# The second feed-forward product by the seven-product scheme at two levels, computed transposed, with operand sums on GpSimd

## The chip, the cores and the metric

The kernel runs on one core of a Trainium2 chip. The metric is the device time of one execution in microseconds (us). The engines are TensorE (PE, with its weight loads PEld), VectorE (DVE), ScalarE (ACT), GpSimd (POOL) and SyncE (SP), whose queue issues nearly all DMAs.

## The reference

One layer of an encoder on x of 2048 tokens x 1024 channels, all float32:

```
h   = rmsnorm(x, g_mix);  p = h @ w_in
y_f = rmsnorm(re(fft2 of 8 groups of 64 channels of p), g_fourier)
y_h = rmsnorm(hyena_mix(the other channels of p), g_hyena)      # two gated long convolutions
x   = x + concat(y_f, y_h) @ w_out
hm  = rmsnorm(x, g_mlp)
a   = square(relu(hm @ w_fc1))        # 2048 x 4096
x   = x + a @ w_fc2                   # 4096 x 1024
out = rmsnorm(x, g_final)
```

The change concerns `x + a @ w_fc2` and the last norm.

## The kernel before

The stages follow one another: input projection, Fourier and long convolutions, output projection, first feed-forward product (`fc1`), second (`fc2`). A scheduler orders the instructions of each engine by data and by the order in which the code is written; each engine then runs its list in order and waits on semaphores. SP's list holds the loads in the order in which they are issued.

A float32 product is made of three matmuls (`mm3`): each operand is split into a high part of reduced precision and the rest, `hi = cast(x)` on ScalarE and `lo = x - hi` on VectorE (`split`), and hi*hi + lo*hi + hi*lo are summed in PSUM.

Both feed-forward products use the seven-product scheme of two-by-two blocks, which saves one product in eight for some sums of blocks. In `fc2` the tokens are taken in two blocks of 1024 (`blk`). In each, the blocks of the scheme are two halves of 512 tokens, two halves of the 4096 inner channels and two halves of 512 output columns. The products are called `m1` to `m7`. The sums of `a` are made by `fc1` and stored in DRAM (`ad[blk][n]`, a0m1 to a1m7 in the trace), those of `w_fc2` were made early in the kernel (`td`). `fc2` therefore only loads: `fetch` brings tiles `ra` (128 x 1024) and `rb` (128 x 1024), eight steps ahead; `prepare` splits each into qah, qal, qbh, qbl (L196, L197); `use` multiplies. The tokens are the stationary side (128 x 128) and 512 output columns the moving one. The result p2u, p2m or p2v is added to the residual `acc` (L1374), and `finish` applies the norm and stores. GpSimd works in this stage only at the very end (L1345), and `fc1` begins its first two products (`begun`) while it ends.

Of the kernel before, what the change touches and what calls it, by code (L numbers as in the profile page):

```python
# [10 lines left out]
F32 = mybir.dt.float32  # L11
FR = mybir.dt.float32r
BF16 = mybir.dt.bfloat16
# [3 lines left out]
EPS = 1e-5  # L17
# [117 lines left out]
def hybrid_block(ctx: ExitStack, tc: tile.TileContext, A, out):  # L135
# [5 lines left out]
    def scratch(name, shape):  # L141
        return dram.tile(shape, F32, tag=name, name=name)
# [12 lines left out]
    ad = [{n: scratch(f"a{i}{n}", [16, P, 512]) for n in ORDER} for i in range(2)]  # L155

    td = scratch("td", [P, 16, 4, 512])

    cpool = ctx.enter_context(tc.tile_pool(name="cpool", bufs=1))
    ps = ctx.enter_context(tc.tile_pool(name="ps", bufs=2, space=PSUM))  # L160
# [6 lines left out]
    def psum(name):  # L167

        banks["stack"].close()
        banks["other"] = banks["stack"].enter_context(tc.tile_pool(name=name, bufs=1, space=PSUM, reuse_waits="tile"))  # L170
        banks["two"] = name == "psd"

    def pa(nm):
        banks["n"] += 1
# [33 lines left out]
    def mm3(o, lh, ll, rh, rl, start, stop, more=False):  # L208

        a = nc.tensor.matmul(o, lhsT=lh, rhs=rh, start=start, stop=False, skip_group_check=more)  # L210
        nc.tensor.matmul(o, lhsT=lh, rhs=rl, start=False, stop=False, skip_group_check=more)  # L211
        return a, nc.tensor.matmul(o, lhsT=ll, rhs=rh, start=False, stop=stop, skip_group_check=more)  # L212
# [946 lines left out]
    def fc2_rows(blk, n, g):  # L1159

        f, f2 = slice(2 * g, 2 * g + 2), slice(2 * g + 16, 2 * g + 18)
        b = {
            "m1": w2v[:, f, left],
            "m2": w2v[:, f2, left],
            "m3": w2v[:, f2, right],
            "m4": td[:, f, 2],
            "m5": td[:, f, 0],
            "m6": td[:, f, 3],
            "m7": td[:, f, 1],
        }  # L1170
        return ad[blk][n][f].rearrange("f p t -> p f t"), b[n]

    def fc2_product(p, j, a, b, start):
        tk = slice(128 * j, 128 * j + 128)
        for g in range(2):
            mm3(p, a[0][:, g, tk], a[1][:, g, tk], b[0][:, g, :], b[1][:, g, :], start and g == 0, g == 1, not start)

    def fc1(mp, rp, zp, b, first, following, begun):

# [103 lines left out]
        fc2_begun = {}  # L1283
        for i, n in enumerate(("m1", "m2")):
            parts = []
            for j, v in enumerate(fc2_rows(0, n, 0)):
                t = rp[:, 2 * i + j, :].rearrange("p (f c) -> p f c", f=2)
                nc.sync.dma_start(t, v)
                parts.append((zf[:, 4 * i + 2 * j], zf[:, 4 * i + 2 * j + 1]))
                split(*parts[j], t)  # L1290
            fc2_begun[n] = [pa("p2" + "um"[i]) for _ in range(4)]
            for j, p in enumerate(fc2_begun[n]):
                fc2_product(p, j, *parts, True)
        return fc2_begun

    def fc2(mp, blk, gfin, begun):

        out_t = out.rearrange("(p t) d -> p t d", t=NT)

        todo = {  # L1300
            "m1": ("u", True, (0, 0)),
            "m2": ("m", True, (0, 0)),
            "m6": ("u", False, (0, 1)),
            "m5": ("v", True, (1, 1)),
            "m3": ("v", False, (0, 1)),
            "m7": ("u", False, (1, 1)),
            "m4": ("u", False, (1, 0)),
        }
        steps = [(g, n, e) for g in range(4) for n in todo for e in range(2)]
        if begun:  # L1310
            steps = [(0, n, e) for e in range(2) for n in ("m1", "m2")] + steps[4:]
        held, raws, parts, acc = {}, {}, {}, {}

        def fetch(k):
            if k < len(steps) and not (begun and k < 2):
                g, n, e = steps[k]
                raws[k] = [load(mp, tag, [P, 2, 512], v, bufs) for (tag, bufs), v in zip((("ra", 10), ("rb", 11)), fc2_rows(blk, n, 2 * g + e))]

        def prepare(k):
            if k in raws:  # L1320
                parts[k] = []
                for side, t in zip("ab", raws.pop(k)):
                    hl = [mp.tile([P, 2, 512], FR, tag="q", name=f"q{side}{h}{steps[k][1]}", bufs=16) for h in "hl"]
                    split(*hl, t)
                    parts[k].append(hl)

        def residual(t0):
            for t in range(t0, t0 + 4):
                acc[t] = load(mp, "acc", [P, 1024], x2d[:, 8 * blk + t, :], 12)

        junk = mp.tile([P, 1024], BF16, tag="mjunk", name="mjunk")

        def finish(i):
            t = acc[i]
            r = rms(t, 1024, junk, "o")
            nc.vector.scalar_tensor_tensor(out=t, in0=t, scalar=r, in1=gfin, op0=ALU.mult, op1=ALU.mult)
            nc.sync.dma_start(out_t[:, 8 * blk + i, :], t)

        ssq = {}

        def squares(i, c):

            s = small.tile([P, 1], F32, tag="ssq", name="ssq_l")
            nc.scalar.activation(junk[:, c], acc[i][:, c], AF.Square, accum_out=s)
            nc.gpsimd.tensor_mul(acc[i][:, c], acc[i][:, c], gfin[:, c])  # L1345
            return s

        def finish_last(i):
            s, v = squares(i, left), small.tile([P, 1], F32, tag="var", name="v_l")
            nc.vector.tensor_add(s, s, ssq[i])  # L1350
            nc.vector.tensor_scalar(out=v, in0=s, scalar1=1.0 / 1024, scalar2=EPS, op0=ALU.mult, op1=ALU.add)
            r = rsqrt(v, small, "s")
            for c, queue in ((right, nc.scalar), (left, nc.sync)):
                t = acc[i][:, c]
                if queue is nc.scalar:
                    nc.scalar.mul(t, t, r)
                else:
                    nc.vector.tensor_scalar(out=t, in0=t, scalar1=r, scalar2=None, op0=ALU.mult)
                queue.dma_start(out_t[:, 8 * blk + i, c], t)

        def use(k, j):
            g, n, e = steps[k]
            bank, start, (rows, cols) = todo[n]
            if k in parts:
                if start and e == 0:
                    held[bank, j] = pa(f"p2{bank}")
                fc2_product(held[bank, j], j, *parts[k], start and e == 0)
            else:
                held[bank, j] = begun[n][j]
            if e == 0:  # L1370
                return
            i = j + 4 * rows
            t = acc[i][:, 512 * cols : 512 * cols + 512]
            nc.vector.tensor_add(t, t, held[bank, j])  # L1374
            if g == 3 and blk == 1 and i in (6, 7):

                if n == "m7":
                    ssq[i] = squares(i, right)
                elif n == "m4":
                    finish_last(i)  # L1380
            elif g == 3 and n in ("m3", "m4"):
                finish(i)

        AHEAD = 8
        with tc.high_priority(offset=300):
            for k in range(5 if begun else 4):
                fetch(k)
            residual(0)
            for k in range(5 if begun else 4, AHEAD):
                fetch(k)  # L1390
            for k in range(4):
                prepare(k)
        tail = 4 if blk else 0
        for k in range(len(steps) - tail):
            fetch(k + AHEAD)
            prepare(k + 2)
            if k == 3:
                residual(4)
            for j in range(4):
                use(k, j)  # L1400
            yield

        for k in range(len(steps) - tail, len(steps)):
            prepare(k)
        for j in range(5 if tail else 0):
            for k, t in ((len(steps) - 4, j), (len(steps) - 3, j), (len(steps) - 2, j - 1), (len(steps) - 1, j - 1)):
                if 0 <= t < 4:
                    use(k, t)
        yield

    def run(*steps):
# [106 lines left out]
        zstack.close()  # L1518
    with pool("fc2") as mp:

        mp.tile([P, 2, 512], F32, tag="ra", name="ra", bufs=10)
        mp.tile([P, 2, 512], F32, tag="rb", name="rb", bufs=11)
        mp.tile([P, 2, 512], FR, tag="q", name="q", bufs=16)
        mp.tile([P, 1024], BF16, tag="mjunk", name="mjunk")
        mp.tile([P, 1024], F32, tag="gfin", name="gfin")
        mp.tile([P, 1024], F32, tag="acc", name="acc", bufs=12)
        gfin = load(mp, "gfin", [P, 1024], A["g_final"].broadcast_to([P, 1024]))
        for blk in range(2):
            run(fc2(mp, blk, gfin, {} if blk else begun))


# [42 lines left out]
```

## Time and profile before

| what | value |
|---|---|
| runs | 2251.12, 2251.25, 2245.84 us; median 2251.12 |
| the profiled execution | 2246.41 us, span 2244.6 us |
| busy in the span | PE 2193.4 us (98%), DVE 1472.5 (66%), ACT 1075.1 (48%), POOL 770.8 (34%) |
| the second product | from 1620.2 us to the end |

In a row of groups stand line, engine, operation, out<-in, shapes, count, then busy us, mean ns of one, and idle time ahead of them with what ended it. In a row of the timeline stand start (us), length (us), engine, line, operation. Lengths include time in which the instruction waits inside the engine. Matmuls overlap, so their distance, not their length, is their cost.

### The profile page before, as it was taken

How to read it: one execution, taken by the hardware profiler on the slowest of the kernel's cores; microseconds unless marked ns; L12 is line 12 of the kernel's file. 1: busy time of each engine (PE TensorE's matmuls, PEld its weight loads, DVE VectorE, ACT ScalarE, POOL GpSimd, SP SyncE). 2: the span in 40 equal slices, each digit the busy share in tenths (PEclk: the TensorE clock that was granted, in tenths of full speed). 3: DMA queues.
4: the chain of work that ended last, by engine and by line, in shares of the span. 5: the costliest groups of instructions: out<-in, count | busy, mean ns of one | idle time of the engine just before them, and what ended most of it. 6: DMA issues, size and time to landing. Idle time of an engine off the chain costs nothing.

```text
span 2244.6 us, 34527 instructions
## 1 busy us (share of the span) xinstructions
PE 2193.4 (98%) x12881; PEld 1794.5 (80%) x12881; DVE 1472.5 (66%) x2196; ACT 1075.1 (48%) x1788; POOL 770.8 (34%) x583
## 2 busy tenths in 40 slices
PE   8999899999999999999999999999999999999998
PEld 6888788676888778887888878888888888888886
DVE  7998767775788864566444474444477666866667
ACT  6555211354556645556555565555443333533333
POOL 3444332454366501337555556555200000000000
PEclk9999999999999999999999999999999999999999
DMA  7535897669898756586444475444498756866631
GB/s 268 178 132 171 313 320 254 208 227 336 304 306 257 237 154 180 175 270 192 153 154 155 155 248 162 150 153 155 160 369 298 248 190 190 308 196 188 200 110 75
DMA packets 289081, 477.00 MB, mean 213 GB/s; under 512 B 17605, under 2 KB 133519, under 8 KB 284177
## 3 DMA queue, kind: packets, MB, share of 16 engines
q1 hardware_dynamic: 282961, 459.34, 61.4%
q10 hardware_dynamic: 5952, 15.46, 2.1%
q8 instruction: 101, 1.65, 0.3%
q14 instruction: 67, 0.55, 0.1%
HBM read 313.56 MB, written 168.00 MB: 215 GB/s over the span
## 4 chain that ended last, share of the span: by engine, by line
PE 89%; ACT 3%; DVE 3%; POOL 2%; issue 2%; DMA 1%; SPq 0%; ACTq 0%; POOLq 0%; DVEq 0%
PE p2u L212 5%; PE p2u L211 5%; PE p2u L210 5%; PE pu L211 5%; PE pu L212 5%; PE pu L210 5%; PE p1u L210 5%; PE p1u L212 5%; PE p1u L211 5%; PE pk L667 3%; PE p2v L211 3%; PE p2v L212 3%; PE p2v L210 3%; PE pz L779 2%; PE p1v L210 2%; PE p1v L211 2%
## 5 line engine op out<-in xcount | busy, mean ns | idle before, releaser
L196 ACT CAST qahm<-ra 128x1024 fp32r<-128x1024 f32 x110 | 115.9, 1053 | 346.7 <-PE p2u L211 172.0
L197 DVE TENSOR_TENSOR qalm<-ra,qahm 128x1024 fp32r<-128x1024 f32 x110 | 134.6, 1224 | 154.7 <-ACT qahm L196 151.8
L1345 POOL TENSOR_TENSOR acc<-acc,gfin 128x512 f32<-128x512 f32 x4 | 5.1, 1277 | 631.6 <-DMA out<-acc 624.4
L211 PE MATMUL pu<-wl,xh 128*128 128x512 f32 x512 | 200.9, 392 | 6.9 <-DVE wl L197 6.5
L210 PE MATMUL pu<-wh,xh 128*128 128x512 f32 x512 | 203.7, 398 | 1.0 <-ACT wh L199 1.0
L212 PE MATMUL pu<-wh,xl 128*128 128x512 f32 x512 | 200.7, 392 | 0.0
L211 PE MATMUL p2u<-qblm,qahm 128*128 128x512 f32 x504 | 196.1, 389 | 0.0
L210 PE MATMUL p2u<-qbhm,qahm 128*128 128x512 f32 x504 | 195.9, 389 | 0.0
L212 PE MATMUL p2u<-qbhm,qalm 128*128 128x512 f32 x504 | 195.8, 389 | 0.0
L197 DVE TENSOR_TENSOR qblm<-rb,qbhm 128x1024 fp32r<-128x1024 f32 x110 | 134.0, 1218 | 0.8 <-ACT qbhm L196 0.7
L412 POOL TENSOR_TENSOR acc<-acc,cw 128x512 f32<-128x512 f32 x45 | 59.8, 1330 | 196.0 <-DVE acc L389 192.6
L196 ACT CAST ahm<-s 128x512 fp32r<-128x512 f32 x124 | 76.8, 621 | 100.2 <-PE p1v L211 54.8
L197 POOL TENSOR_TENSOR alm<-W,ahm 128x512 fp32r<-128x512 f32 x63 | 88.8, 1410 | 92.2 <-ACT ahm L196 92.2
L211 PEld LDWEIGHTS pu<-wl,xh 128*128 128x128 f32 x512 | 97.0, 189 | 28.3 <-DVE wl L197 6.9
L196 ACT CAST qbhm<-rb 128x1024 fp32r<-128x1024 f32 x110 | 115.4, 1049 | 3.1 <-DMA rb<-in_w_fc 1.9
L210 PEld LDWEIGHTS pu<-wh,xh 128*128 128x128 f32 x512 | 96.8, 189 | 22.1 <-ACT wh L199 1.8
L212 PEld LDWEIGHTS pu<-wh,xl 128*128 128x128 f32 x512 | 96.7, 189 | 20.6 <-DVE xl L197 0.6
L210 PEld LDWEIGHTS p2u<-qbhm,qahm 128*128 128x128 f32 x504 | 94.6, 188 | 20.1 <-issue 0.3
L211 PEld LDWEIGHTS p2u<-qblm,qahm 128*128 128x128 f32 x504 | 94.6, 188 | 19.6
L212 PEld LDWEIGHTS p2u<-qbhm,qalm 128*128 128x128 f32 x504 | 94.6, 188 | 19.4
L210 PE MATMUL p1u<-bm,ahm 128*128 128x512 f32 x252 | 99.0, 393 | 4.6 <-ACT ku L1207 4.6
L196 ACT CAST ahm<-W 128x512 fp32r<-128x512 f32 x94 | 58.1, 621 | 94.7 <-PE p1u L211 90.6
(376 smaller groups left out, 6141.6 us busy)
## 6 DMA issues: line engine op xcount, KB each, us to landing
W<-in_w_fc SPq DMA_DIRECT2D x66, 512.0 KB, 4.7
ks<-spec SPq DMA_DIRECT2D x64, 512.0 KB, 4.7
rb<-td SPq DMA_DIRECT2D x64, 512.0 KB, 10.9
ra<-a1m SPq DMA_DIRECT2D x56, 512.0 KB, 3.7
ra<-a0m SPq DMA_DIRECT2D x54, 512.0 KB, 3.8
rb<-in_w_fc SPq DMA_DIRECT2D x46, 512.0 KB, 5.2
f<-in_w_fc SPq DMA_DIRECT2D x16, 1024.0 KB, 8.5
td<-f SPq DMA_DIRECT2D x16, 1024.0 KB, 5.9
```

Of the source, the lines that this page charges most:

```text
L196: nc.scalar.copy(hi, src)
L197: (eng or nc.vector).tensor_sub(lo, src, hi)
L210: a = nc.tensor.matmul(o, lhsT=lh, rhs=rh, start=start, stop=False, skip_group_check=more)
L211: nc.tensor.matmul(o, lhsT=lh, rhs=rl, start=False, stop=False, skip_group_check=more)
L212: return a, nc.tensor.matmul(o, lhsT=ll, rhs=rh, start=False, stop=stop, skip_group_check=more)
L412: nc.gpsimd.tensor_add(m1, m1, cw[:, 3, :])
L667: ordered(nc.tensor.matmul(p[:, 128 * j : 128 * j + 128], lhsT=f2[:, 4 * q + j, :], rhs=self.G[:, :, 4 * q + j], start=True, stop=True))
L779: nc.tensor.matmul(p[:, 256 * sp : 256 * sp + 256], lhsT=e1[:, sp, :], rhs=zz[:, :, lo : lo + 16], start=True, stop=True)
L1345: nc.gpsimd.tensor_mul(acc[i][:, c], acc[i][:, c], gfin[:, c])
```

## The change

`fc2` applies the scheme twice. The seven products of before are now the inner ones, called `inner`: for each, the operands are no longer multiplied, but cut in two-by-two blocks again: tokens by `blk` (0 or 1, 512 each), inner channels into two halves of 1024, output columns into two halves of 256. Each inner product takes seven outer products (`outer`), 49 in all. The tiles of an inner product are h11, h21 (block 0, first and second half of its channels), h12, h22 (block 1), and w1, w2 (the two channel halves of the weights); each has 4 chunks j, of 128 x 1024 for h and 128 x 2 x 512 for w, whose columns `first` and `second` are the two output halves. There is one buffer of each, so the next inner product's chunk is loaded once the last user of this one has read it.

The sums of the second level are made in the kernel from these tiles: for each of the 4 chunks four on tokens (128 x 1024) and four on weights (128 x 512), on GpSimd; of the first inner product, eight of the weights' sums are on VectorE.

A step is one chunk of one outer product: 2 channel groups x 2 weight tiles x 3 = 12 matmuls. The weights are now the stationary side and 512 tokens the moving one, so the result is transposed; `turned` turns it back on TensorE ahead of the addition to the residual. `evict` takes the result of an outer product out of PSUM into u11 to u22 in SBUF, by an addition on VectorE (a copy where there is nothing to add to). Sums that several inner products share go to DRAM and come back (`sumd`), and finished columns go to `x3d` until a row is complete. `fc1` begins three steps of the first outer product instead of two products.

```diff
-    def fc2_product(p, j, a, b, start):
-        tk = slice(128 * j, 128 * j + 128)
-        for g in range(2):
-            mm3(p, a[0][:, g, tk], a[1][:, g, tk], b[0][:, g, :], b[1][:, g, :], start and g == 0, g == 1, not start)
+    def fc2_product(p, w, h, start):
+        for k in range(2):
+            for j in range(2):
+                c = slice(128 * j, 128 * j + 128)
+                mm3(p[j], w[0][:, k, c], w[1][:, k, c], h[0][:, k, :], h[1][:, k, :], start and k == 0, k == 1, not start)
...
+        inner = ("m1", "m2", "m6", "m5", "m3", "m7", "m4")
+        outer = ("m1", "m2", "m6", "m5", "m7", "m3", "m4")
+        h = {n: mp.tile([P, 4, 2, 512], F32, tag=f"h{n}", name=f"h{n}") for n in ("11", "12", "21", "22", "t2")}
+        w = {n: mp.tile([P, 4, 2, 512], F32, tag=f"w{n}", name=f"w{n}") for n in "12"}
+        s2 = mp.tile([P, 4, 2, 256], F32, tag="s2", name="s2")
...
+        def token_sums(n, j, eng):
+            b11, b12, b21, b22, t2 = (h[k][:, j] for k in ("11", "12", "21", "22", "t2"))
+            if n == 3:
+                eng.tensor_sub(b12, b22, b12)
+            elif n == 2:
+                eng.tensor_add(t2, b12, b11)
+            elif n == 1:
+                eng.tensor_sub(b11, b22, t2)
+            else:
+                eng.tensor_sub(b21, b21, t2)
+
+        def weight_sums(n, j, eng):
+            a11, a21, a12, a22 = (w[k][:, j, :, c] for k in "12" for c in (first, second))
+            if n == 3:
+                eng.tensor_sub(a21, a11, a21)
+            elif n == 2:
+                eng.tensor_sub(s2[:, j], a22, a21)
+            elif n == 1:
+                eng.tensor_add(a11, s2[:, j], a11)
+            else:
+                eng.tensor_sub(a12, a12, s2[:, j])
+
+        operands = {
+            "m1": (w["1"], first, "11"),
+            "m2": (w["2"], first, "21"),
+            "m6": (s2, slice(0, 256), "t2"),
+            "m5": (w["1"], first, "11"),
+            "m7": (w["1"], second, "12"),
+            "m3": (w["2"], first, "22"),
+            "m4": (w["2"], second, "21"),
+        }
+
+        def prepare(s):
+            if 3 <= s < 28 * len(inner):
+                j = s % 4
+                a, c, b = operands[outer[s // 4 % 7]]
+                hh, hl = (mp.tile([P, 2, 512], FR, tag="qh", name=f"qh{n}", bufs=8) for n in "hl")
+                wh, wl = (mp.tile([P, 2, 256], FR, tag="qw", name=f"qw{n}", bufs=8) for n in "hl")
+                split(hh, hl, h[b][:, j])
+                split(wh, wl, a[:, j, :, c])
+                parts[s] = (wh, wl), (hh, hl)
...
+        def evict(e, q, add, p):
+            t = held[e, q]
+            for j in range(2):
+                if add:
+                    nc.vector.tensor_add(t[:, j], p[j], t[:, j])
+                else:
+                    nc.scalar.copy(t[:, j], p[j])
+
+        def turned(t, j):
+            p = pa("pt_o")
+            for k in range(4):
+                nc.tensor.transpose(p[:, 128 * k : 128 * k + 128], t[:, j, 128 * k : 128 * k + 128], ident)
+            return p.rearrange("p (k f) -> p k f", k=4)
...
+        LOADS = {"1": -12, "12": -10, "22": -10, "11": -7, "2": -5, "21": -3}
+        SUMS = {3: (-7, -6, -4, -3), 2: (-1, 0, 2, 3), 1: (5, 6, 8, 9), 4: (11, 12, 14, 15)}
+        for i in range(len(inner)):
+            for n, r in LOADS.items():
+                for j in range(4):
+                    if i:
+                        at(28 * i + r + j, fetch, i, n, j)
+            for n, rs in SUMS.items():
+                for j, r in enumerate(rs):
+                    if i or n in (1, 4):
+                        at(28 * i + r, token_sums, n, j, nc.gpsimd)
+                        at(28 * i + r, weight_sums, n, j, nc.gpsimd)
+                    else:
+                        at(3 + j, token_sums, n, j, nc.gpsimd)
+                        at(5 + j, weight_sums, n, j, nc.vector)
...
+        for s in range(3, total):
...
+            prepare(s + 3)
...
+            fc2_product(bank[b], *parts.pop(s), start)
+            if j < 3:
+                continue
+            for e, (src, dest) in enumerate(ends[n]):
...
+                evict(e, q, src or (done and o != "m4"), bank[b])
+                if done:
+                    deliver(s, e, q, dest)
```

`LOADS` and `SUMS` say at which step of an inner product (negative: of the one before) a load or a sum is written in the code; data alone decides when it runs.

GpSimd's list in the second product. Before, it ends with the last sums and splits of `fc1` and four multiplications:

```order
L197 TENSOR_TENSOR alm_15251<-s_15233,ahm_15250 128x512
L197 TENSOR_TENSOR alm_15255<-W,ahm_15254 128x512
L1345 TENSOR_TENSOR acc<-acc,gfin 128x512 x4
L1570 UNCONDITIONAL_BRANCH
L1570 ISA
```

Now, from the middle of one inner product's sums to the next one's:

```order
L1337 TENSOR_TENSOR ht2_15649<-h12_15646,h11_15645 128x1024
L1348 TENSOR_TENSOR s2_15652<-w2_15651,w1_15650 128x512 x3
L1339 TENSOR_TENSOR h11_15645<-h22_15648,ht2_15649 128x1024
L1350 TENSOR_TENSOR w1_15650<-s2_15652,w1_15650 128x2x256
...
L1341 TENSOR_TENSOR h21_15647<-h21_15647,ht2_15649 128x1024
L1352 TENSOR_TENSOR w2_15651<-w2_15651,s2_15652 128x2x256
...
L1346 TENSOR_TENSOR w1_15650<-w1_15650 128x2x256 x4
L1335 TENSOR_TENSOR h12_15646<-h22_15648,h12_15646 128x1024
L1337 TENSOR_TENSOR ht2_15649<-h12_15646,h11_15645 128x1024
```

Each of L1335, L1337, L1339, L1341, L1346, L1348, L1350 and L1352 comes four times in an inner product: 112 sums of 128 x 1024 and 104 of 128 x 512 stand on this list where there were none.

VectorE's list in the second product, before: the low parts of one step's two tiles, and additions of p2u to the residual.

```order
L197 TENSOR_TENSOR qalm6_15688<-ra_15635,qahm6_15687 128x1024
L197 TENSOR_TENSOR qblm6_15692<-rb_15637,qbhm6_15691 128x1024
L1374 TENSOR_TENSOR acc_15639<-acc_15639,p2u_15549 128x512
L1374 TENSOR_TENSOR acc_15641<-acc_15641,p2u_15550 128x512
L1374 TENSOR_TENSOR acc_15639<-acc_15639,p2m_15583 128x512
```

Now, around the eviction of `m1` and `m2` of one inner product (h21 and w2 are the operands of `m2`, ht2 and s2 those of `m6`, h11 and w1 those of `m5`):

```order
L199 TENSOR_TENSOR qhl_17718<-h21_15647,qhh_17717 128x1024
L199 TENSOR_TENSOR qwl_17720<-w2_15651,qwh_17719 128x512
L1385 TENSOR_TENSOR u11_17658<-p2u_17660,u11_17658 128x512 x2
L199 TENSOR_TENSOR qhl_17740<-h21_15647,qhh_17739 128x1024
L199 TENSOR_TENSOR qwl_17742<-w2_15651,qwh_17741 128x512
...
L199 TENSOR_TENSOR qhl_17806<-ht2_15649,qhh_17805 128x1024
L199 TENSOR_TENSOR qwl_17808<-s2_15652,qwh_17807 128x512
L1385 TENSOR_TENSOR u11_17658<-p2m_17747,u11_17658 128x512
L1385 TENSOR_TENSOR u11_17658<-p2m_17748,u11_17658 128x512
L199 TENSOR_TENSOR qhl_17831<-ht2_15649,qhh_17830 128x1024
L199 TENSOR_TENSOR qwl_17833<-s2_15652,qwh_17832 128x512
```

The low parts are now a 128 x 1024 and a 128 x 512 for each step, 193 of each, and an eviction stands ahead of the last step's low parts of the following outer product.

More of the change, by code (lines that the diff above doesn't have):

```diff
@@ new lines, in fc1 @@
+        room = {n: work.wp.tile([P, 32, 128], F32, tag=n, name=f"first{n}", bufs=2).rearrange("p (n f) c -> p n (f c)", n=4) for n in "GV"}
+        psum("psd2")
+        u = pair("p2u")
+        u = [u[:, j, :] for j in range(2)]
+        for j in range(3):
+            raw = rp[:, 2 * j : 2 * j + 2] if j < 2 else room["V"][:, 0:2]
+            raw = [raw[:, k].rearrange("p (f c) -> p f c", f=2) for k in range(2)]
+            rows = fc2_rows(0, "m1", j)
+            for t, v in zip(raw, rows):
+                nc.sync.dma_start(t, v)
+            h = (zf[:, 3 * j], zf[:, 3 * j + 1]) if j < 2 else [room["G"][:, k].bitcast(FR).rearrange("p (f c) -> p f c", f=2) for k in range(2)]
+            w = zf[:, 3 * j + 2] if j < 2 else room["G"][:, 2].bitcast(FR).rearrange("p (f c) -> p f c", f=2)
+            w = [w[:, k].rearrange("p (f c) -> p f c", f=2) for k in range(2)]
+            split(*h, raw[0])
+            split(*w, raw[1][:, :, 0:256])
+            fc2_product(u, w, h, j == 0)
```

279 lines of the change are left out of this document (166 added, 113 removed).

## Prediction

> **What bounds the kernel now.** I read the page first, its busy shares and its chain of waits, and then the last stage alone, since only that stage is rewritten.
>
> ```profile
> span 2244.6 us, 34527 instructions
> PE 2193.4 (98%) x12881; PEld 1794.5 (80%) x12881; DVE 1472.5 (66%) x2196; ACT 1075.1 (48%) x1788; POOL 770.8 (34%) x583
> ...
> PE 89%; ACT 3%; DVE 3%; POOL 2%; issue 2%; DMA 1%; SPq 0%; ACTq 0%; POOLq 0%; DVEq 0%
> ```
>
> TensorE holds 89% of the chain. The table by stretches (busy us and counts of PE, weight loads, DVE, ACT, POOL; clock; DMA share; GB/s) gives the second product, its first part and its last 9.6 us:
>
> ```profile
> 1620.20:1700.00 79.80, 79.80 (x353) 65.77 (x352) 55.66 (x64) 31.77 (x32) 0.00 (x0) 1.00 0.99 362
> ...
> 1620.20:2240.00 619.80, 615.56 (x2714) 508.89 (x2712) 431.81 (x549) 242.91 (x275) 5.04 (x4) 1.00 0.65 216
> 2235.00:2244.60 9.60, 0.76 (x4) 0.29 (x2) 3.72 (x15) 3.18 (x8) 2.52 (x2) 0.68 0.43 165
> ```
>
> TensorE is busy 615.6 of 619.8 us, VectorE 70%, GpSimd 5 us. In the list of waits ScalarE, which makes the high parts, waits for TensorE to give buffers back, so everything else runs ahead of TensorE:
>
> ```profile
> ACT qahm L196 <- PE p2u L211: 172.0, 52, 3.4
> ```
>
> The timeline of TensorE has a matmul every 0.2267 us (12 of them from 2232.65 to 2235.37, 2.72 us):
>
> ```profile
> 2232.65 0.39 PE L212 MATMUL p2u<-qbhm,qalm 128*128 128x512 f32 x1
> ...
> 2235.37 0.39 PE L212 MATMUL p2u<-qbhm,qalm 128*128 128x512 f32 x1
> ```
>
> **What the change takes from TensorE.** Before: 2 blocks x 7 products x 16 chunks x 4 token tiles x 3 = 2688 matmuls. After: 49 products x 8 chunks x 2 weight tiles x 3 = 2352. The 336 removed are worth 336 x 0.2267 = 76.2 us while TensorE is the bound. Turning the result back adds 128 transposes; the timeline shows 8 of the same kind in a row between 1003.93 and 1004.72, 0.10 us each, so 13 us.
>
> ```profile
> 1003.93 1.04 PE L247 MATMUL pt_m<-ident,hm 128*128 128x128 f32 x8
> 1004.72 0.47 PE L210 MATMUL p1u<-zf,ebhm 128*128 128x512 f32 x1
> ```
>
> If TensorE stayed the bound, the stage would lose 63 us.
>
> **What it adds elsewhere.** Call 12 matmuls a step (one chunk pair of one product): 196 steps, 28 for each of the 7 inner products. Each step needs one split of a 128x1024 tile and one of 128x512: on ScalarE two casts, on VectorE two subtractions. And each inner product needs 16 token sums (128x1024) and 16 weight sums (128x512) on GpSimd. The groups by shape:
>
> ```profile
> L196 ACT CAST qahm<-ra 128x1024 fp32r<-128x1024 f32 x110 | 115.9, 1053 | 346.7 <-PE p2u L211 172.0 <-PE p2v L211 106.7 <-PE p2m L211 44.6
> ...
> L196 ACT CAST ahm<-s 128x512 fp32r<-128x512 f32 x124 | 76.8, 621 | 100.2 <-PE p1v L211 54.8 <-PE p1m L211 24.5 <-PE p1u L211 12.6
> ```
>
> ```profile
> L197 DVE TENSOR_TENSOR qalm<-ra,qahm 128x1024 fp32r<-128x1024 f32 x110 | 134.6, 1224 | 154.7 <-ACT qahm L196 151.8 <-issue 2.7 <-DMA ra<-a0m 0.2
> ...
> L1374 DVE TENSOR_TENSOR acc<-acc,p2u 128x512 f32<-128x512 f32 x128 | 84.8, 680 | 12.5 <-PE p2u L212 12.3
> ```
>
> ```profile
> L608 POOL TENSOR_TENSOR acc<-acc,sqr 128x512 f32<-128x512 f32 x56 | 71.7, 1280 | 66.7 <-ACT sqr L604 49.7 <-ACT acc L604 15.0
> ...
> L610 POOL TENSOR_TENSOR acc<-acc 128x256 f32<-128x256 f32 x8 | 5.8, 730 | 0.6
> ```
>
> ScalarE needs 1.05 + 0.62 = 1.67 us a step against 2.72: covered. Its copies out of PSUM are two for each of four quarters at the very first inner product: nothing. A 128x1024 sum on GpSimd has no row. From 256 to 512 columns it grows by 0.55 us, so another 512 cost 1.10 and the sum 2.38 us; two of the 512 kind, 2.58, is the upper end, and 2 x 730 = 1.46, if the growth flattened, the lower. I take 2.38, for the line goes through both rows.
>
> Alone, GpSimd's sums are 16 x (2.38 + 1.28) = 58.6 us for an inner product, whose steps take TensorE 28 x 2.72 = 76.2. Taken engine by engine all would be covered. It is not, because of the next view.
>
> **VectorE and GpSimd take turns.** Both timelines of the first product, where both engines add tiles in SBUF:
>
> ```profile
> 1443.16 1.63 DVE L1220 TENSOR_TENSOR s<-c 128x512 f32<-128x512 f32 x1 [1.36 <-ACT c L1146]
> 1444.83 0.69 DVE L1221 TENSOR_TENSOR s<-s,c 128x512 f32<-128x512 f32 x1
> 1445.43 0.69 DVE L197 TENSOR_TENSOR alm<-s,ahm 128x512 fp32r<-128x512 f32 x1
> 1446.04 0.69 DVE L1222 TENSOR_TENSOR c<-c 128x512 f32<-128x512 f32 x1
> 1446.64 1.78 DVE L1223 TENSOR_TENSOR s<-c,s 128x512 f32<-128x512 f32 x1
> 1450.18 0.69 DVE L1142 TENSOR_TENSOR c<-p1v,ku 128x512 f32<-128x512 f32 x1 [1.76 <-ACT ku L1207]
> ```
>
> ```profile
> 1442.95 1.29 POOL L1133 TENSOR_TENSOR s<-s,W 128x512 f32<-128x512 f32 x1
> 1446.20 1.67 POOL L1134 TENSOR_TENSOR s<-W 128x512 f32<-128x512 f32 x1 [1.96 <-DVE alm L197]
> 1447.84 1.74 POOL L197 TENSOR_TENSOR alm<-s,ahm 128x512 fp32r<-128x512 f32 x1
> 1449.65 1.29 POOL L1135 TENSOR_TENSOR s<-W,s 128x512 f32<-128x512 f32 x1
> ```
>
> L1220 starts inside L1133, which ends at 1444.24, and ends at 1444.79: 0.55 us after it, instead of 0.69 after its own start. L1134 starts inside L1222, which ends at 1446.73, and ends 1.14 later. L1142 reads one operand from PSUM, lies wholly across two GpSimd sums, and keeps 0.69. So a VectorE instruction with two SBUF operands and a GpSimd sum exclude each other, and one with a PSUM operand is free. Where both have work queued they alternate one for one:
>
> ```profile
> 1334.26 4.55 DVE L197 TENSOR_TENSOR bm<-bm 128x1024 fp32r<-128x1024 f32 x2
> ```
>
> ```profile
> 1333.75 1.74 POOL L1132 TENSOR_TENSOR s<-W 128x512 f32<-128x512 f32 x1 [0.68 <-DVE s L1220]
> 1335.57 2.16 POOL L1133 TENSOR_TENSOR s<-s,W 128x512 f32<-128x512 f32 x1
> 1337.69 2.27 POOL L197 TENSOR_TENSOR alm<-W,ahm 128x512 fp32r<-128x512 f32 x1
> ```
>
> Two 128x1024 subtractions took 4.55 us instead of 2.4, and GpSimd's 1.28 became 2.16 and 2.27: 1.15 of its own plus 1.08 of VectorE's. These four are the shared costs: GpSimd 1.15 (512) and 1.15 + 1.10 = 2.25 (1024), VectorE 0.55 and 1.08. The splits all have two SBUF operands; the evictions (`evict`, the adds after `turned`) read PSUM and are free. Before, the stage had nothing on GpSimd but four multiplications at its end.
>
> [...]
>
> **The sum.** For one inner product the shared port is asked for 16 x (2.25 + 1.15) = 54.4 us by GpSimd and 28 x (1.08 + 0.55) = 45.6 by VectorE: 100 us against TensorE's 76.2. Over a cycle of 28 steps it is not always in use. In data's order GpSimd's 32 sums begin when the `m3` operand h22 has been split and reloaded (about step 22) and follow each other from there. Alternating, VectorE gets 32 turns, 16 steps, meanwhile: 54.4 + 16 x 1.63 = 80.5 us, 5.0 a step; TensorE starves. Then GpSimd has nothing for 12 steps, until the next h22. These take between VectorE's time, 12 x (1.13 + 0.60) = 20.8 (starts 2189.22 to 2190.35 below, 1444.83 to 1445.43 above) and its share of 128 PSUM adds, 8 x 0.62 = 5, so 25.8, and TensorE's, 12 x 2.72 = 32.6; halfway, since VectorE may only be three steps ahead (`prepare(s + 3)`, and the eviction waits for TensorE ahead of the next split), 29.2.
>
> ```profile
> 2189.22 1.22 DVE L197 TENSOR_TENSOR qblm<-rb,qbhm 128x1024 fp32r<-128x1024 f32 x1
> ...
> 2190.35 1.28 DVE L1374 TENSOR_TENSOR acc<-acc,p2u 128x512 f32<-128x512 f32 x2
> ```
>
> A cycle is 110 us; seven are 770. Ahead of them lie the loads: SP issues 24 of 0.5 MB, of which the first ten (5.2 MB, at the 362 GB/s of the first stretch 14 us) must land before `m6` can have sums, with the begun steps covering a little: 12 us. The end: last eviction, four transposes, squares, root, stores: before, 9.2 us from the last matmul; now more small instructions, with four rows finished ahead of the last eviction on VectorE: 15. The reloaded sums (`sumd`) and residuals go over SP, where this stage has a DMA share of 0.65 now with 220 operand loads of 0.5 MB and has 168 of them after: covered.
>
> 1620.2 + 770 + 12 + 15 = 2417.2 for the span, and 1.8 us around it as in the profiled execution (2246.4 against a span of 2244.6): 2419. That execution is 4.7 us under the median of 2251.1 shown; I say 2420, 173 us slower.
>
> Bounds: a port that never idles, 7 x 100 + 12 + 9: 2343. Unshortened durations (GpSimd 58.6, VectorE 16 x 1.91, TensorE's 32.6: 122 a cycle) with start and end as taken: 2503.
>
> **Rivals.**
> - *TensorE stays the bound; faster.* The splits pass freely beside the sums, or VectorE's queued splits always go first. Then 2246.4 - 63 + 12 + 6 = 2201. It decides where GpSimd's and VectorE's port time fall under 2.72 us a step; they ask for 3.57, so a sum would have to cost about half of any row. Against it: L1220, L1223 and the 4.55 us. 0.06.
> - *The port never idles:* GpSimd's sums are spread over the cycle by waits for loads, so the free part vanishes. 2343. For it: the order shows weight sums held back until w2 is reloaded. 0.12.
> - *TensorE's clock falls.* In the alternating part it waits about 2.3 us a step. A wait of 2.83 us brought half clock here:
>
> ```profile
> 1329.24 0.50 PE L210 MATMUL p1u<-bm,ahm 128*128 128x512 f32 x1 [2.83 <-ACT ku L1207]
> 1331.33 0.63 PE L211 MATMUL p1u<-bm,ahm 128*128 128x512 f32 x1
> 1331.76 0.63 PE L212 MATMUL p1u<-bm,alm 128*128 128x512 f32 x1
> ```
>
> ```profile
> 1330.00:1334.00 4.00, 4.00 (x12) 3.10 (x12) 3.50 (x4) 4.00 (x6) 1.54 (x2) 0.57 0.93 254
> ```
>
> The granted clock of these 4 us is 0.57. At 0.43 us a matmul a step takes 5.2, over the 5.0 that VectorE delivers: up to 16 x 0.2 and some 4 us to recover, 7 to 8 a cycle: 2475. 0.12.
> - *No difference:* stalls that happen to equal the 63 us saved; 0.02. *Beyond 2503:* loads late on SP behind stores that wait for evictions; 0.03.
>
> **Chances.** The forecast case has 0.65. Slower by over 0.3% (what a measurement of this kernel can tell from none): 0.65 + 0.12 + 0.12 + 0.03 = 0.92; within, 0.02; faster, 0.06. The range of 2335 to 2500 takes in both bounds and the clock.
>
> **What the profile after would show.** Stage from 1620 to about 2417; GpSimd busy well over 58 us a cycle with its 128x1024 sums near 3 us in the mean; the 128x1024 subtractions near 2 us in the mean instead of 1.22; TensorE idle for VectorE's low parts, five-microsecond steps alternating with stretches at full rate, some seven times. It is wrong if those subtractions keep 1.22 us beside the sums, or if TensorE is busy 95% there.

## The result, and the profile after

The changed kernel takes 2452.85 us, median of four runs (2445.93 to 2456.71), against 2251.18 for the kernel before beside it (2245.84 to 2253.4): 1.0896 times as long, with a 95% interval of 1.0865 to 1.0927. The forecast was 2420, between 2335 and 2500. The profiled execution is the shortest of the four, 2445.93 us, with a span of 2444.1.

The head of the page, busy time by engine and the shares of the chain that ended last:

```profile
span 2444.1 us, 34756 instructions
PE 2218.3 (91%) x12673; PEld 1782.2 (73%) x12673; DVE 1801.1 (74%) x2275; ACT 1163.6 (48%) x1983; POOL 1292.3 (53%) x803
...
PE 67%; DVE 16%; issue 6%; DMA 5%; POOL 3%; ACT 3%; SPq 0%; DVEq 0%; ACTq 0%; POOLq 0%
```

TensorE's share of the chain fell from 89% to 67%, VectorE's rose from 3% to 16%. The table by stretches (busy us and counts of PE, weight loads, DVE, ACT, POOL; clock; DMA share; GB/s) gives one stretch in which GpSimd has sums, one in which it has none, the last 14.6 us, and the whole second product:

```profile
1835.20:1919.80 84.60, 65.90 (x268) 52.08 (x266) 83.92 (x53) 32.40 (x42) 76.08 (x32) 0.88 0.49 163
1919.80:1942.40 22.60, 22.22 (x98) 18.21 (x98) 20.88 (x26) 12.16 (x17) 0.04 (x2) 1.00 0.61 201
...
2429.50:2444.10 14.60, 0.66 (x4) 0.42 (x4) 6.44 (x20) 6.09 (x21) 0.00 (x0) 0.58 0.57 216
1620.00:2444.10 824.10, 642.43 (x2515) 497.32 (x2513) 762.06 (x630) 333.63 (x471) 528.36 (x224) 0.89 0.52 177
```

While GpSimd has sums, VectorE is busy 83.92 of 84.60 us and TensorE is not: it issued 268 matmuls (24 of them transposes), where at one each 0.2267 us it could have issued 373. When GpSimd is quiet TensorE is busy 22.22 of 22.60. The groups by shape over the stage:

```profile
L199 DVE TENSOR_TENSOR qhl<-h,qhh 128x1024 fp32r<-128x1024 f32 x165 | 330.4, 2003 | 29.3 <-ACT qhh L198 29.2
L199 DVE TENSOR_TENSOR qwl<-w,qwh 128x512 fp32r<-128x512 f32 x165 | 236.3, 1433 | 2.4 <-ACT qwh L198 2.4
...
L1337 POOL TENSOR_TENSOR ht<-h,h 128x1024 f32<-128x1024 f32 x28 | 84.0, 3001 | 2.1
...
L1385 DVE TENSOR_TENSOR u<-p2u,u 128x512 f32<-128x512 f32 x56 | 35.6, 675 | 0.0
```

The 128x1024 subtraction takes 2.00 us in the mean instead of 1.22 and GpSimd's sum 3.00, while the VectorE addition with a PSUM operand keeps its 0.68. The two timelines show the turns:

```profile
1859.83 3.40 DVE L199 TENSOR_TENSOR qhl<-h,qhh 128x1024 fp32r<-128x1024 f32 x1
1863.15 2.83 DVE L199 TENSOR_TENSOR qwl<-w,qwh 128x512 fp32r<-128x512 f32 x1
```

```profile
1859.31 2.83 POOL L1335 TENSOR_TENSOR h<-h,h 128x1024 f32<-128x1024 f32 x1
1862.23 3.21 POOL L1337 TENSOR_TENSOR ht<-h,h 128x1024 f32<-128x1024 f32 x1
```

L1335 ends at 1862.14 and the subtraction that began inside it 1.09 us later, at 1863.23; L1337 ends at 1865.44 and the subtraction of 128x512 0.54 us later. These are the shared costs that the forecast used (1.08 and 0.55).

### The profile page after: what moved, and what is told of

Its sections match the earlier page's. It is cut to its first block, busy times and chain, and to the rows that moved or that the text cites. A ratio compares the mean times of both kernels' runs of the same rounds, so it can differ in the third digit from the quotient of the medians.

```text
span 2444.1 us, 34756 instructions
## 1 busy us (share of the span) xinstructions
PE 2218.3 (91%) x12673; PEld 1782.2 (73%) x12673; DVE 1801.1 (74%) x2275; ACT 1163.6 (48%) x1983; POOL 1292.3 (53%) x803
## 4 chain that ended last, share of the span: by engine, by line
PE 67%; DVE 16%; issue 6%; DMA 5%; POOL 3%; ACT 3%; SPq 0%; DVEq 0%; ACTq 0%; POOLq 0%
DVE qhl L199 6%; DVE qwl L199 5%; PE pu L213 5%; PE pu L214 5%; PE pu L212 5%; PE p1u L212 4%; PE p1u L213 4%; PE p1u L214 4%; PE pk L669 2%; PE pz L781 2%; PE p2u L214 2%; PE po L212 2%; PE po L214 2%; PE po L213 2%; PE pz L788 2%
## 5 line engine op out<-in xcount | busy, mean ns | idle before, releaser
L199 DVE TENSOR_TENSOR qhl<-h,qhh 128x1024 fp32r<-128x1024 f32 x165 | 330.4, 2003 | 29.3 <-ACT qhh L198 29.2
L198 ACT CAST qhh<-h 128x1024 fp32r<-128x1024 f32 x165 | 173.4, 1052 | 319.4 <-PE p2u L213 200.7
L199 DVE TENSOR_TENSOR qwl<-w,qwh 128x512 fp32r<-128x512 f32 x165 | 236.3, 1433 | 2.4 <-ACT qwh L198 2.4
L214 PE MATMUL p2u<-qhh,qwl 128*128 128x512 f32 x436 | 185.4, 425 | 35.3 <-DVE qwl L199 33.5
L212 PE MATMUL p2u<-qhh,qwh 128*128 128x512 f32 x436 | 183.5, 421 | 16.3 <-ACT qwh L198 10.7
L213 PE MATMUL p2u<-qhl,qwh 128*128 128x512 f32 x436 | 184.0, 422 | 9.2 <-DVE qhl L199 9.2
L214 PEld LDWEIGHTS p2u<-qhh,qwl 128*128 128x128 f32 x436 | 88.7, 203 | 66.7 <-DVE qwl L199 48.2
L1346 POOL TENSOR_TENSOR w<-w 128x512 f32<-128x512 f32 x24 | 37.3, 1557 | 163.1 <-DMA w<-td 118.8
L212 PEld LDWEIGHTS p2u<-qhh,qwh 128*128 128x128 f32 x436 | 89.6, 205 | 36.1 <-ACT qwh L198 11.5
L213 PEld LDWEIGHTS p2u<-qhl,qwh 128*128 128x128 f32 x436 | 89.2, 205 | 34.4 <-DVE qhl L199 15.7
L198 ACT CAST qwh<-w 128x512 fp32r<-128x512 f32 x165 | 101.4, 615 | 14.1 <-PE p2u L213 6.6
```

Source lines behind the costliest of these rows:

```text
L198: nc.scalar.copy(hi, src)
L199: (eng or nc.vector).tensor_sub(lo, src, hi)
L1346: eng.tensor_sub(a21, a11, a21)
```

## The experiments

The theory: a GpSimd sum and a VectorE instruction with two SBUF operands cannot run together, and by taking turns the sums stretch the splits until VectorE, not TensorE, sets the pace. Against it stand the sums' waits and GpSimd's own time, the loads, TensorE's clock, and a bound by total demand (the sum of both engines' shared costs) instead of by turns. All kernels are edits of the changed one.

**No sums.** The loop that places the sums is empty; `m6` reads two tiles that are loaded instead of `s2` and `ht2`.

```diff
...
-                for j, r in enumerate(rs):
+                for j, r in enumerate(()):
...
```

> The kernel after without the 216 GpSimd sums and the 8 on VectorE (operands are multiplied unsummed, m6 takes h12 and w2 instead of the sums). Turn-taking theory (splits on VectorE and sums on GpSimd exclude each other): with the sums gone a cycle of 28 steps falls from 111 us to TensorE's 76 plus 2 for the transposes, the stage ends near 2200 to 2230, 128x1024 subtractions back at 1.22 us. Rival, loads and single buffers set the pace and the sums only fill waits: above 2350.

Measured: 2225.8 us, one run, beside 2247.91 for the kernel before.

**Sums that only write.** Each sum becomes memsets of the same destination, several of them so that GpSimd is busy about as long. The order stays, and so do the waits for the tile that each overwrites; the waits for tiles that a sum only reads are gone with the reads.

```diff
...
-                eng.tensor_sub(b12, b22, b12)
...
+            eng.memset(dst, 0.5)
+            eng.memset(dst, 0.5)
+            eng.memset(dst[:, 0], 0.5)
...
```

> Each GpSimd sum is replaced by memsets of the same destination that take GpSimd about as long (128x1024: two whole and one half; 128x512: two whole and a quarter), so GpSimd has its chain, its time and its consumers, but reads nothing; values are constants. Turn-taking over reads: subtractions stay at 1.22 us, total within 20 us of the run without sums. Rival, GpSimd's chain of about 58 us a cycle is late for the steps by itself: near 2450. Rival, any GpSimd instruction excludes the subtractions: near 2450 too, but with the 128x1024 subtractions near 2.0 us in the mean.

Measured: 2223.58 us, one run. The stretch 1660 to 2180 of this kernel, and two of its groups over the whole stage:

```profile
1660.00:2180.00 520.00, 515.35 (x2296) 425.61 (x2297) 423.11 (x544) 304.34 (x405) 351.80 (x622) 0.99 0.74 252
```

```profile
L199 DVE TENSOR_TENSOR qhl<-h,qhh 128x1024 fp32r<-128x1024 f32 x165 | 203.3, 1232 | 83.5 <-ACT qhh L198 83.4
...
L1337 POOL MEMSET h<- 128x1024 f32 x84 | 79.7, 950 | 118.5 <-DVE qhl L199 74.1 <-DMA h<-a1m 44.4
```

GpSimd is busy 351.80 of the 520 us and waits for loads and splits here too, yet the subtraction is back at 1.23 us and TensorE at 515 of 520. So neither GpSimd's time nor these waits cost anything. The waits that went with the reads cannot be the loss either: in the changed kernel VectorE is busy 495 of the same 520 us (its row stands below, under the warm TensorE), and the time is lost in its stretched instructions. What costs is that the sums read SBUF; the whole loss, 2452.9 - 2224 = 229 us, comes with that.

**All sums on VectorE, and the token sums alone on VectorE.** In the first `nc.gpsimd` becomes `nc.vector` for every sum; in the second for the token sums only, and all weight sums are on GpSimd.

```diff
-                        at(28 * i + r, token_sums, n, j, nc.gpsimd)
-                        at(28 * i + r, weight_sums, n, j, nc.gpsimd)
+                        at(28 * i + r, token_sums, n, j, nc.vector)
+                        at(28 * i + r, weight_sums, n, j, nc.vector)
...
```

> All sums on VectorE, GpSimd empty in the stage. Turn-taking theory: VectorE has 28 x 1.73 + 16 x 1.73 + 18 x 0.62 = 87 us a cycle with nothing to wait for, against 111 measured: 7 x 24 less, about 2285 (2260 to 2310). Rival, VectorE is simply full (99% busy in the alternating parts) and more work on it costs its own time: 2453 + 7 x 27.7 = 2645.

> Token sums (128x1024) on VectorE, all weight sums (128x512) on GpSimd. Turn-taking: the shared port is asked for 28 x 1.63 + 16 x 1.08 + 16 x 1.15 = 81 us a cycle, VectorE alone for 28 x 1.73 + 16 x 1.13 + 11 = 78, and what is not hidden behind its PSUM adds comes on top: 81 to 96 a cycle, near 88, about 2285. If it is well under the run with all sums on VectorE, GpSimd's help is worth having for the small sums; if over, none is.

Measured: 2306.88 us (ratio to before 1.0257, 1.024 to 1.0274) and 2327.24 (1.0351, 1.0333 to 1.037). With all sums on it, VectorE is busy 518 of 520 us:

```profile
1660.00:2180.00 520.00, 483.08 (x2022) 371.14 (x2022) 517.98 (x648) 260.98 (x344) 0.00 (x0) 0.98 0.65 222
```

Giving VectorE more work made the kernel 146 us faster: on GpSimd a sum cost VectorE more than the sum itself. The second to fifth inner products took 84 to 88 us each (from every 336th matmul to the next), near VectorE's time; the last two took 104 and 108, where the finished rows come in between and ScalarE waits for them in order:

```profile
ACT mjunk L239 <- DMA fin<-x3d: 59.1, 8, 10.4
```

The second was expected to tie with the first and is 20 us slower, so even the small sums are better on VectorE. A part of the reason shows in its timelines of GpSimd (two rows, the second of which the first takes in) and of VectorE, and in ScalarE's waits:

```profile
1919.04 22.26 POOL L1348 TENSOR_TENSOR s<-w,w 128x512 f32<-128x512 f32 x2 [0.84 <-DMA w<-td]
...
1929.71 11.59 POOL L1348 TENSOR_TENSOR s<-w,w 128x512 f32<-128x512 f32 x1
```

```profile
1926.77 1.22 DVE L199 TENSOR_TENSOR qhl<-h,qhh 128x1024 fp32r<-128x1024 f32 x1
1927.90 0.68 DVE L199 TENSOR_TENSOR qwl<-w,qwh 128x512 fp32r<-128x512 f32 x1
1928.50 1.28 DVE L1385 TENSOR_TENSOR u<-p2u,u 128x512 f32<-128x512 f32 x2
1929.70 1.21 DVE L1337 TENSOR_TENSOR ht<-h,h 128x1024 f32<-128x1024 f32 x1
```

```profile
ACT qwh L198 <- POOL s L1348: 23.5, 4, 8.2
```

Two weight sums of 1.28 us took 22.26 together. VectorE's instructions follow each other without a gap and keep 1.22 and 0.68: no turn is given. The first sum ended when VectorE worked on the pair L1385, which reads PSUM, since the second began at 1929.71. The second ended at 1941.30, with VectorE's next such pair:

```profile
1940.05 1.28 DVE L1385 TENSOR_TENSOR u<-p2u,u 128x512 f32<-128x512 f32 x2
```

Here the wait falls on GpSimd, and the casts of the weight sums wait behind it (23.5 us).

**Loads earlier.** Only places in SBUF are exchanged.

```diff
+            ("w1", ...), ("u", ...), ("w2", ...), ("h11", ...), ("h21", ...),
             ("h12", [P, 4, 2, 512], F32, 1),
             ("h22", [P, 4, 2, 512], F32, 1),
...
-            ("h21", ...), ("w2", ...), ("h11", ...), ("w1", ...),
```

> Only the places of the tiles in SBUF are exchanged: h11, w1, h21 and w2, which the first loads fill, stand where the first product has nothing left after 1624, and h12, h22 where h11 and w2 stood. In the changed kernel SyncE waits 18.8 us, to 1636.9, for a store out of a tile s of the first product before it issues the first operand load, and GpSimd's first sum starts at 1651.0. If it is that store's buffer which keeps the loads back, the first load is issued near 1624 and the first splits follow at about 1632; h12 and h22 still come at 1637, so the first sum starts at about 1642, and the time falls by 8 to 10 us, to about 2443. If the loads are kept back by the data (a1m) or by the DMA's rate, the first sum stays at 1651 and the time at 2453. The alternation from there on is unchanged by both.

Measured: 2447.83 us (ratio 1.0893, 1.0873 to 1.0913): the intervals overlap with the changed kernel's, so no gain is shown. SyncE's timeline of the changed kernel, then of this one, then its first sum:

```profile
1636.93 0.36 SPq L1330 DMA_DIRECT2D h<-a0m  x1
```

```profile
1626.69 0.36 SPq L1330 DMA_DIRECT2D h<-a0m  x1
1627.10 0.46 SPq L1328 DMA_DIRECT2D w<-in_w_fc  x1
1632.88 0.36 SPq L1330 DMA_DIRECT2D h<-a0m  x1
1640.39 0.37 SPq L1328 DMA_DIRECT2D w<-in_w_fc  x1
...
1641.89 1.05 SPq L1330 DMA_DIRECT2D h<-a1m  x2
```

```profile
1651.63 2.34 POOL L1335 TENSOR_TENSOR h<-h,h 128x1024 f32<-128x1024 f32 x1 [45.80 <-PE p2m L213]
```

The first load moved 10 us forward, of the 13 expected, but the fourth now waits to 1640.39 for matmuls that still read the new place of `w2`, and the loads of `h12` and `h22` stand behind it in the queue. The first sum stayed where it was. That the old place of a tile keeps the loads back is shown; how much of the start a better arrangement would save is open.

**TensorE kept warm.** Four more matmuls in each step of the alternating part.

```diff
+            if s % 28 in (*range(17, 28), *range(9)):
+                for x in range(4):
+                    nc.tensor.matmul(bank[b][x % 2], lhsT=wh[:, x // 2, 0:128], rhs=hh[:, x // 2, :], start=False, ...)
```

> Four more matmuls after the twelve of each step in steps 17 to 27 and 0 to 8 of every inner product, which add a product a second time (the output is another). They keep TensorE busy in its gaps: 16 x 0.2267 = 3.63 us of the 4.2 us that a step of the alternating part takes. In the changed kernel the granted clock is half for 188 us of the stage. If that costs time (the rival of my prediction), the clock goes back to 1.0 and the time falls, by up to 188 / 2 = 94 us. If VectorE's share of the port sets the pace and TensorE waits for it at any clock, half-clock time goes to near 0 and the time stays at 2453 within 10 us.

Measured: 2463.03 us (2461.48 and 2464.58). The stretch 1660 to 2180 of the changed kernel, then of this one:

```profile
1660.00:2180.00 520.00, 411.55 (x1566) 315.68 (x1567) 495.14 (x332) 206.74 (x266) 373.19 (x157) 0.88 0.49 163
```

```profile
1660.00:2180.00 520.00, 454.86 (x1902) 361.92 (x1902) 495.20 (x330) 205.86 (x266) 375.04 (x156) 0.95 0.49 165
```

The clock rose from 0.88 to 0.95, short of 1.0, and VectorE did the same work in the same time (332 and 330 instructions, 495 us). The time that the throttle granted half clock in this stretch fell from 124 to 51 us, and the kernel did not get faster: it took 10 us longer, which stays unexplained. TensorE's clock is not what sets the pace.

**Token sums alone, weight sums alone.** The first leaves out the weight sums, the second the token sums; in each, `m6` reads a loaded tile in place of the sum that is missing.

```diff
...
                         at(28 * i + r, token_sums, n, j, nc.gpsimd)
-                        at(28 * i + r, weight_sums, n, j, nc.gpsimd)
...
```

```diff
...
-                        at(28 * i + r, token_sums, n, j, nc.gpsimd)
                         at(28 * i + r, weight_sums, n, j, nc.gpsimd)
...
```

> The 16 weight sums of each inner product are left out (m6 reads another weight tile); the 16 token sums of 128x1024 stay on GpSimd. Theory A, one for one: 16 sums take turns with 16 subtractions, 8 steps, 16 x 2.25 + 8 x 1.63 = 49 us in which TensorE needs 22; some 8 us of that is made up from the steps prepared ahead, the other 20 steps run at TensorE's rate, so a cycle is about 49 + 54 - 8 = 95 against 77 without sums, and the time is 2226 + 7 x 18 = 2352. Theory B, only the total demand on the port counts: 36 + 45.6 = 81.6 us a cycle, 2226 + 7 x 5 = 2261. Theory C, GpSimd's sums delay VectorE by a fixed amount each, half of the sums gone takes half of the loss: 2340; C is told from A by the next run.

> The 16 token sums of each inner product are left out (m6 reads another token tile); the 16 weight sums of 128x512 stay on GpSimd. Theory A, one for one: 16 x 1.15 + 8 x 1.63 = 31.4 us for 8 steps in which TensorE needs 21.8; of the 9.6 lost some 8 are made up from the steps prepared ahead: 2226 + 7 x 2 = 2240, between 2226 and 2290. Theory B, total demand: 18.4 + 45.6 = 64 us, under TensorE's 76: 2226. Theory C, a fixed delay for each sum whatever its size, half of the loss: 2340.

Measured: 2356.03 us (2354.22 and 2357.85) and 2234.3 us (2233.47 and 2235.13).

```profile
1660.00:2180.00 520.00, 444.36 (x1807) 341.43 (x1808) 485.64 (x394) 235.94 (x306) 265.89 (x93) 0.94 0.55 188
```

```profile
1660.00:2180.00 520.00, 506.50 (x2251) 415.09 (x2251) 492.52 (x533) 295.91 (x390) 181.98 (x102) 0.99 0.72 243
```

The count by turns gave 2352 and 2240; total demand 2261 and 2226; a fixed delay 2340 for both. Only the turns fit both. The weight sums alone cost 8 to 11 us over the kernel without sums and the one whose sums only write (one run each); by the count the steps prepared ahead cover most of what they take.

**Smaller turns.** Each token sum is cut into four instructions of 128x256.

```diff
+            for g in range(4):
-            b11, b12, b21, b22, t2 = (h[k][:, j] for k in ("11", "12", "21", "22", "t2"))
+                b11, b12, b21, b22, t2 = (h[k][:, j, g // 2, 256 * (g % 2) : 256 * (g % 2) + 256] for k in ("11", "12", "21", "22", "t2"))
```

> The changed kernel with each token sum on GpSimd written as four of 128x256 instead of one of 128x1024; nothing else differs, and no work is left out. One for one: a turn of GpSimd is then 0.60 (0.73 for 128x256 less the 0.13 that is not shared) for the token sums and 1.15 for the weight sums, 80 turns an inner product; every one of VectorE's 56 subtractions waits for one such turn and none for more, so nothing is left of the free part, GpSimd is busy through the whole cycle, and the cycle is what both ask of the port, 16 x 4 x 0.60 + 16 x 1.15 + 45.6 = 102, up to 108 with the 5% by which the alternating part exceeded its sum: 2453 - 7 x (110 - 105) = 2418, between 2397 and 2440. The mean of the 128x1024 subtractions stays near 2 us while that of the 128x512 ones rises or stays. If instead GpSimd keeps the port while it has instructions queued, or each of its instructions costs VectorE a fixed wait, four times as many cost more: 2500 or beyond.

Measured: 2418.9 us (2417.08 to 2426.2; ratio 1.0768, 1.0738 to 1.0799), 34 us less than with whole sums, with the same work.

```profile
1660.00:2180.00 520.00, 426.92 (x1662) 324.33 (x1662) 426.48 (x351) 214.52 (x278) 505.46 (x401) 0.91 0.53 176
```

```profile
L199 DVE TENSOR_TENSOR qhl<-h,qhh 128x1024 fp32r<-128x1024 f32 x165 | 262.3, 1590 | 35.7 <-ACT qhh L198 35.3
L199 DVE TENSOR_TENSOR qwl<-w,qwh 128x512 fp32r<-128x512 f32 x165 | 207.5, 1259 | 12.6 <-ACT qwh L198 12.5
```

GpSimd is now the busy one, 505 of 520 us, with hardly a pause between its sums. But the means of the two subtractions were expected to stay or rise, and fell to 1.59 and 1.26 us: VectorE is no longer full (426 of 520) and waits for ScalarE, which waits for sums. So the time came out in the middle of the expected range, 2397 to 2440, but one sign of its reasoning failed, and that it lies within 1 us of the 2418 computed is in part luck. From the busy shares the limit is now GpSimd's own pace beside VectorE's turns; no run tests that further.

**Token sums on VectorE, no weight sums.** As in the second kernel above, without the weight sums.

```diff
-                        at(28 * i + r, token_sums, n, j, nc.gpsimd)
-                        at(28 * i + r, weight_sums, n, j, nc.gpsimd)
+                        at(28 * i + r, token_sums, n, j, nc.vector)
...
```

> The token sums stand on VectorE and the weight sums are left out (m6 reads another weight tile), so GpSimd reads nothing beside VectorE. VectorE's work of an inner product is 28 x (1.13 + 0.60) + 16 x 1.13 + 8 x 0.68 + 3 = 75 us against 76.2 of TensorE: if VectorE's time and nothing else counts, the time is that without any sums and a little more, 2226 to 2245, and a version that made the weight sums before this stage could end at or just under the 2248 of the kernel before. If in-order waits on VectorE (a sum that waits for its load holds the splits behind it) cost as much as in the kernel with all sums on VectorE, whose last two inner products took 104 and 108 us, it ends at 2260 to 2280, and no placing of the sums on VectorE wins.

Measured: 2248.15 us (ten runs, 2242.67 to 2252.82) against 2248.59, ratio 0.9996 (0.9985 to 1.0008).

```profile
1660.00:2180.00 520.00, 502.78 (x2209) 407.43 (x2209) 509.58 (x619) 287.25 (x381) 0.00 (x0) 0.99 0.71 241
```

The time lies between the two ranges that were expected. VectorE is busy 509.58 of 520 us, and still TensorE is busy 502.78: the first five inner products end at 2038.2 us, no later than without any sums (2041.2). The 22 us over that kernel come in the last two, 90.1 and 102.9 us instead of 81.4 and 86.7, where ScalarE waits for the finished rows. Its wait in these two (2038 to 2231 us), then the same in the kernel without sums (2041 to 2209):

```profile
ACT mjunk L239 <- DMA fin<-x3d: 48.7, 8, 10.2
```

```profile
ACT mjunk L239 <- DMA fin<-x3d: 4.2, 3, 2.1
```

So with the weight sums made elsewhere at no cost, this arrangement draws level with the kernel before; whether the finished rows can be placed so that the 22 us go was not tried. With the token sums made elsewhere and the weight sums on GpSimd, 2234.3 us (ratio 0.9935, 0.9915 to 0.9955) would be left, before the price of making them. No version with all of its sums beat the kernel before; without any sums it would lie 1% below.

## Why the prediction was right, step by step

- **The turns** are shown. Reads by GpSimd's sums stretch VectorE's splits (no sums 2225.8, sums that only write 2223.6, sums that read 2452.9): the 128x1024 subtraction takes 2.00 us in the mean beside sums that read SBUF and 1.23 beside those that only write it, while the addition with a PSUM operand keeps 0.68. The prediction calls what the two engines take in turns a port; no run shows one. The runs show the turns and their costs, 1.08 and 0.55 us of VectorE.
- **The start was mis-sized: 12 us taken, 31 measured.** The first sum began at 1650.96. I let the operand loads begin at 1620, as those of before did. SyncE waited 18.8 us for a store out of a tile of the first product, whose place the new tiles take:

```profile
SPq L1330 <- DMA a1m<-s: 18.8, 1, 18.8
```

```profile
1650.96 2.39 POOL L1335 TENSOR_TENSOR h<-h,h 128x1024 f32<-128x1024 f32 x1 [45.77 <-DMA h<-a1m]
```

  From the first load at 1636.93 to the first sum are 14.0 us, the time that I had computed for the loads themselves. With that wait gone (loads earlier, above) the first sum stayed at 1651.63, so how much of it could be saved is open.
- **The cycles: 770 us taken, 778.5 measured** (1651.0 to the last matmul's end at 2429.5). From the first sum of one inner product to that of the next, the five in the middle took 107 to 115 us, 110.0 in the mean, which is the cycle that was taken. The first took 73, with 24 sums on GpSimd, and the last 155, to the last matmul. That the mean is met so well is luck, since both halves of a cycle were off by amounts that cancel. In the cycle shown above the alternating part was 84.6 instead of 80.5 and the free part 22.6 instead of 29.2, together 107.2. What was off in the first half is that the 32 sums were taken to follow each other: GpSimd is busy 76.08 of the 84.60 us and waits in the rest, mostly for loads of weights. VectorE goes on in these pauses at its own length (its timeline, then GpSimd's):

```profile
1842.87 1.21 DVE L199 TENSOR_TENSOR qhl<-h,qhh 128x1024 fp32r<-128x1024 f32 x1
1844.00 0.68 DVE L199 TENSOR_TENSOR qwl<-w,qwh 128x512 fp32r<-128x512 f32 x1
```

```profile
1845.23 1.82 POOL L1346 TENSOR_TENSOR w<-w 128x512 f32<-128x512 f32 x1 [2.83 <-DMA w<-td]
```

  So it made 18 and 19 subtractions beside the 32 sums (17 + 1 and 18 + 1 below) instead of 16 and 16, and 54.4 + 18 x 1.08 + 19 x 0.55 = 84.3. The turns themselves are one for one: of the 173 second-level sums in the changed kernel that began within 0.15 us of another's end, 157 have exactly one VectorE instruction with two SBUF operands that ends between that end and their own, 16 have none, and no sum has two.

```profile
L199 DVE TENSOR_TENSOR qhl<-h,qhh 128x1024 fp32r<-128x1024 f32 x17 | 40.8, 2401 | 0.7 <-ACT qhh L198 0.7
L199 DVE TENSOR_TENSOR qwl<-w,qwh 128x512 fp32r<-128x512 f32 x18 | 31.8, 1769 | 0.0
...
L199 DVE TENSOR_TENSOR qhl<-ht,qhh 128x1024 fp32r<-128x1024 f32 x1 | 3.4, 3392 | 0.0
...
L199 DVE TENSOR_TENSOR qwl<-s,qwh 128x512 fp32r<-128x512 f32 x1 | 1.8, 1766 | 0.0
```

- **The end** was 14.6 us, 15 taken. Start and cycles together make up the profiled execution: 2417.2 + 18.8 + 8.5 - 0.4 = 2444.1. The other 7 us between 2420 and the median are those by which that execution is under it.
- **The signs asked for** all came: 128x1024 sums of 2.88 to 3.00 us in the mean of their four lines, subtractions of 2.00, PSUM additions unchanged, seven alternations, and TensorE busy 78% of the stage (642.43 of 824.10 us).
- **A reading that was off:** L1142 lies inside one GpSimd sum (L1135, 1449.65 to 1450.94), not across two. That it keeps 0.69 us beside it stands.
- **Rivals.** The clock did fall (0.88 in the alternating part), yet with less than half of the half-clock time left in the stretch 1660 to 2180 (51 us of 124) nothing was gained (2463 us). No row shows the 4 us to recover that the sum of this rival takes: the clock of 0.57 over the 4 us from 1330 to 1334 amounts to 3.4 us at half clock. The rival in which the port never idles was approached only by smaller turns, at 2419, above the 2343 computed for it. The time of the rival in which TensorE stays the bound was computed too low as well: with nothing in TensorE's way, the kernel without sums takes 2225.8, not 2201.

## What to carry to other kernels

Before work goes to an idle GpSimd, look at what VectorE does at that time: where VectorE's instructions had two SBUF operands and GpSimd's sums read SBUF, their times added, and the same sums were 146 us cheaper on the fuller VectorE. Price it by turns in the stretch where both have work queued, not by total demand over the stage (token sums alone: 2352 by turns, 2261 by total demand, 2356 measured). With each token sum on GpSimd in four smaller instructions the kernel was 34 us faster. The new stage's first load waited 18.8 us for a store out of a tile whose place it takes; look at that too, although the one exchange of places tried here showed no gain.

## What the runs showed of the hardware that was not expected

A GpSimd sum that waited did not always get the next turn. In the changed kernel it did wherever sums were queued (none of the 173 waited for two VectorE instructions, above). With the token sums on VectorE it mostly did too (44 of 55 by the same count waited for one), but there two weight sums took 22.26 us instead of 2.6, and VectorE lost nothing. VectorE instructions that started later went ahead of a GpSimd sum that had already started: ten with two SBUF operands began after the second sum, between 1930.83 and 1939.45, and ended before it. What decides it is open. Both sums ended when VectorE turned to PSUM operands, but that VectorE's instructions follow each other without a gap is not enough to keep GpSimd out. In the same kernel a sum got in between two that do (GpSimd's timeline, then VectorE's):

```profile
1855.62 2.22 POOL L1352 TENSOR_TENSOR w<-w,s 128x512 f32<-128x512 f32 x1 [1.77 <-DVE qwl L199]
```

```profile
1855.47 1.21 DVE L1337 TENSOR_TENSOR ht<-h,h 128x1024 f32<-128x1024 f32 x1
1856.60 2.32 DVE L199 TENSOR_TENSOR qhl<-h,qhh 128x1024 fp32r<-128x1024 f32 x1
```

L1337 ends at 1856.68, the sum 1.16 us later, and the subtraction, which began before L1337's end, 1.08 us after the sum.
